# Spectra stored once and copied in DRAM, tables behind a pass's weights, and earlier copies out of PSUM in a hybrid Fourier/Hyena block on one core

## The chip, the cores and the metric

The kernel runs on one core of a Trainium2 chip. The metric is the device time of one execution in microseconds; smaller is better. Five engines work beside each other, each through its own instructions in order: TensorE (PE, matmuls), VectorE (DVE), ScalarE (ACT), GpSimd (POOL) and SyncE (SP), which here issues most of the transfers (DMAs). An engine waits where an instruction needs a result of another engine or of a transfer that is not there yet.

## The reference

One layer of an encoder on 2048 positions of 1024 channels, in float32:

```
h   = rmsnorm(x)
p   = h @ W_in                       # 2048 columns: Fourier group | x1 | x2 | v, 512 each
y_f = rmsnorm(Re(fft2(p_fourier)))   # 8 groups of 64 channels, over positions and channels
x1, x2, v = short_conv(p_rest)       # three taps over positions
k   = implicit_filters(...) * decay, normalised        # two filters per channel, both directions
z   = v
for n, gate in enumerate((x1, x2)):
    z = gate * (irfft(rfft(z) * rfft(k[:, n])) + z * d[n])
y_h = rmsnorm(z)
x   = x + concat(y_f, y_h) @ W_out
x   = x + relu(rmsnorm(x) @ W_fc1)**2 @ W_fc2
out = rmsnorm(x)
```

## The kernel before

Every product in float32 is made of three matmuls: `split` (L193) rounds an operand to a high half (ACT) and takes the rest as a low half (DVE or POOL), and `mm3` (L208) adds high x high, high x low and low x high in PSUM. So each operand of PE has an ACT cast (`wh`, `ahm`, `yh`) and a subtraction (`wl`, `alm`, `yl`) ahead of it.

The work goes in stages, one after the other on PE.

1. **Pass 1** projects x1 and x2 for 16 tiles of 128 positions and makes the short convolution; **pass 2** projects the Fourier group and v in the same way. Both are `project` (L347). `weights_in` (L314) loads a pass's weights on SP, tile by tile, and splits them. Beside pass 2 the generator `tables` (L1451) loads the tables that later stages need (`e1f`, `e1k`, `turn`, `gy`, `dk8`, `e1z`, `wo`, then `emb` and the Fourier factors `ff`) and forms sums of W_fc2 (`f` to `td`).
2. **Fourier and filters** (`fourier` L490, `filters` L539) are 44 steps. The first eleven carry the second stage of the Fourier transform: `rows(i)` (L499) negates the sine factors on ACT (`neg`), transforms one or two frequencies on PE (L510 to L516), and stores the rows. Eight filter units follow each other four steps apart. A unit generates its filter in four quarters (L584 on PE, times the decay into `k` on DVE, L589; squares on ACT, L603, added up on POOL, L607 to L610), sums over partitions (`psum_k`, L615), takes its first transform (L656, transposed by DVE into `Gk`, L660), and its second (L666), whose result `ks` goes to DRAM in four stores (`spec`, L674). `kd` holds each spectrum twice, as two halves of 64 rows. A unit in `SINGLE` stores it once, and `doubled` (L342) later copies it from DRAM to DRAM (L345). Steps 24 to 27 load `zz` (the convolved v), and `SCALE` tells at which steps DVE multiplies which pieces of it by the filters' norms (L728).
3. **Hyena** (L732): eight blocks, four groups of 128 channels for each of two gates. A block makes the transform of its input (`first`, `second`), multiplies by the spectrum (loaded as `ks`, L764), transforms back (`inverse`, `turn`: DVE transposes V into W) and multiplies by the gate (`gate`, L815). Block by block takes about 25 us. Two of the copies of `doubled` stand in blocks 1 and 2 (one spectrum each, four copies).
4. **Output projection** (`project_out` L964 with the class `Out`): per tile of positions the Fourier rows `yf` are fetched from DRAM in two loads (L917, L919), normalised (`oyn`, L237 and L995), transposed on PE (`pt_y`, L926) and multiplied. `weights` splits W_out (`ost`, into tiles G and V). Some time later the first fc1 weights are loaded into `W` (`fc1_weights`, L1103).
5. **fc1** (`fc1`, L1179): one level of a Strassen-like scheme with seven products m1 to m7 for each of 32 slices of the hidden layer, 16 slices for each half of the positions, so that after iteration 15 all operands change to the other half ("change of blocks"). `keep` (L1205) copies a PSUM sum to SBUF on ACT: `km1` (L1207, in the trace `km`), `ku2` and `ku3` (`ku`), so that the same PSUM tile can take the next product. **fc2** (L1296) has the same scheme.

What sets the order: the program is written tile by tile, and a scheduler places each engine's instructions by when their operands are ready and by priority; `tc.high_priority` moves instructions forward. `behind(later, first)` (L202) forces an instruction to be placed after another one without waiting for it. The lists `line`, `acts`, `fetched`, `stored` and `summed` hold instructions to be placed behind: `acts` the squares of the first four steps and later copies, `fetched` the last load of a spectrum.

Of the kernel before, what the change touches and what calls it, by code (L numbers as in the profile page):

```python
# [10 lines left out]
F32 = mybir.dt.float32  # L11
# [116 lines left out]
P = 128  # L128
# [6 lines left out]
def hybrid_block(ctx: ExitStack, tc: tile.TileContext, A, out):  # L135
    nc = tc.nc
# [174 lines left out]
                    yield  # L311


    def weights_in(wp, sets, stage):  # L314

        w = {}
        for h, s in enumerate(sets):
            src = wfd if s < 0 else A["w_in"][:, (1536, 512, 1024)[s] : (1536, 512, 1024)[s] + 512]
            for k in range(8):
                hi, lo = (wp.tile([P, 512], FR, tag=f"{n}{h}{k}", name=f"{n}{h}{k}") for n in ("wh", "wl"))  # L320
                pl, tag, bufs = stage[(8 * h + k) % len(stage)]
                if tag != "xt":
                    t = pl.tile([P, 512], F32, tag=tag, name="st", bufs=bufs)
                    nc.sync.dma_start(t, src[128 * k : 128 * k + 128, :])
                elif k % 2 == 0:

                    two = pl.tile([P, 2, 512], F32, tag=tag, name="st2", bufs=bufs)
                    nc.sync.dma_start(two, src[128 * k : 128 * k + 256, :].rearrange("(a p) d -> p a d", p=P))
                    t = two[:, 0]
                else:  # L330
                    t = two[:, 1]
                if s < 0:
                    split(hi, lo, t)
                else:
                    split(hi, lo, t, gmix[:, k : k + 1])
                w[h, k] = hi, lo
        return w

    line, acts, fetched, stored, summed = [], [], [], [], []
    SINGLE = (5, 7)  # L340

    def doubled(i, q):  # L342

# [146 lines left out]
    def fourier(fp, uf, e1f, ffs):  # L490
        groups = [(0,)] + [(f, f + 1) for f in range(1, 17, 2)]
        G = fp.tile([P, 128, 32, 2], F32, tag="Gf", name="Gf")
        ufv = uf.rearrange("p t (b j) -> p t b j", b=2)
        for c in range(16):
            p = pa("pf1")
            ordered(nc.tensor.matmul(p, lhsT=e1f, rhs=ufv[:, :, :, 16 * c : 16 * c + 16], start=True, stop=True))
            yield turned(G, c, p.rearrange("p (x c e) -> p c e x", c=8, e=2))

        def rows(i):  # L499

            n, p = len(groups[i]), pa("pf2")
            neg = fp.tile([P, 2, P], F32, tag="neg", name="neg", bufs=2)[:, 0:n]
            behind([nc.scalar.mul(neg, ffs[i][:, :, 1], -1.0)], acts[-1])
            for s, f in enumerate(groups[i]):
                co, si, ns = ffs[i][:, s, 0], ffs[i][:, s, 1], neg[:, s]
                a, b = p[:, 256 * s : 256 * s + 132], p[:, 256 * s + 132 : 256 * s + 256]
                gr, gi = (G[:, :, j].rearrange("p (c j) e -> p c j e", c=2) for j in (f, (16 + f) % 32))
                cos, sin = slice(0, 33), slice(33, 64)
                if f % 16 == 0:
                    ordered(nc.tensor.matmul(a, lhsT=co, rhs=gr[:, :, cos], start=True, stop=True))  # L510
                    ordered(nc.tensor.matmul(b, lhsT=ns, rhs=gr[:, :, sin], start=True, stop=True))
# [12 lines left out]
            def part(c, w):  # L524
                return row[:, :, c : c + 2 * w].rearrange("p s (c j) -> p s c j", c=2)

            nc.vector.tensor_add(part(0, 62), va[:, :, :, 0:62], sb)
            nc.vector.tensor_sub(part(132, 62), va[:, :, :, 0:62], sb)
            for c in (124, 256):
                nc.scalar.copy(part(c, 4), va[:, :, :, 62:66])  # L530
            nc.scalar.copy(row[:, :, 264:388], row[:, :, 0:124])
            nc.sync.dma_start(yfd[:, groups[i][0] : groups[i][0] + n, :], row)

        for i in range(len(groups)):
            rows(i)
            yield


    def filters(ctx, tp, fp, gp, zp, zzs, norms, emb, wo, e1k, f2, dk8, tabs, fourier_steps):  # L539
# [7 lines left out]
        class Unit:  # L547
# [3 lines left out]
            def decay(self, k):  # L551

                if k < 2:
                    decs[k] = fp.tile([P, 8, 128], F32, tag="dec", name="dec", bufs=2)
                elif k == 2:
                    two = tp.tile([P, 2, 8, 128], F32, tag="dec2", name="dec2")
                    decs[2], decs[3] = two[:, 0], two[:, 1]
                d = (nc.scalar if self.i == 0 and k < 2 else nc.sync).dma_start(decs[k], A["decay"][self.ct][:, 8 * k : 8 * k + 8, :])
                if self.i == 0 and k < 2:
                    behind([d], line[0])  # L560

            def generate(self, k):
                self.multiply(k, self.raw(k))
# [121 lines left out]
        SOLO = 11  # L685
        FOURIER = (4, 4, 4, 4, 2, 1, 1, 1, 1, 2, 1)
        LOAD = {24: 0, 25: 1, 26: 2, 27: 3}
        SCALE = {30 + 2 * j + h: [(j, 2 * h), (j, 2 * h + 1)] for j in range(4) for h in range(2)}
        for step in range(44):
            if step == SOLO:  # L690
                yield
# [40 lines left out]
    def hyena(hp, wp, rp, zz, e1, b1, f2, a2, work):  # L732
# [98 lines left out]
        for i in range(8):  # L831
            cur, old, older, new = (blocks[j] if 0 <= j < 8 else None for j in (i, i - 1, i - 2, i + 1))
            for q in range(8):
# [28 lines left out]
                if new:  # L862
                    for c in FIRSTS[q]:
                        new.first(c)
                if i in (1, 2) and q % 2:
                    doubled(SINGLE[i - 1], q // 2)
        old, older = blocks[7], blocks[6]
        for q in range(8 - LAG, 8):
            old.inverse(q)
        for k in range(0, 2):  # L870
            work.weights(hp, k)
        for q in range(4):
            older.gate(q)
        for k in range(2, 4):
            work.weights(hp, k)
        next(ahead)
        for c in range(8):
            old.turn(c)
# [10 lines left out]
    class Out:  # L889
# [20 lines left out]
        def fourier_rows(self, t, pl, tag, bufs, late=None):  # L910

            yf = pl.tile([P, 4, P], F32, tag=tag, name="yf", bufs=bufs)
            if late is not None:
                nc.scalar.copy(yf[:, 0, 0:1], late)
            src = yfd.rearrange("(b q) f c -> q f b c", b=2)
            dst = yf.rearrange("p (b n) c -> p b (n c)", b=2)
            nc.sync.dma_start(dst[0:64], src[:, t, :, 0:256])  # L917

            nc.sync.dma_start(dst[64:128], src[:, 16 - t, :, 132:388] if t else src[:, 16, :, 0:256])  # L919
            return yf.rearrange("p n c -> p (n c)")  # L920

        def parts(self, yn, yh, yl, t=0):
# [180 lines left out]
    def fc1_weights(rp, f, pair, late=None):  # L1103

        r = []
        for j, i in enumerate((f, f + 16)):
            t = rp[:, 2 * pair + j, :].rearrange("p (k f) -> p k f", k=8)
            if late is not None:
                nc.scalar.copy(t[:, 0, 0:1], late)
            nc.sync.dma_start(t, w1v[:, :, 128 * i : 128 * i + 128])  # L1110
            r.append(t)
        return r

# [65 lines left out]
    def fc1(mp, rp, zp, b, first, following, begun):  # L1179
# [24 lines left out]

        def keep(p, nm):  # L1205
            t = mp.tile([P, 512], F32, tag="keep", name=nm, bufs=4)
            nc.scalar.copy(t, p)  # L1207
            return t

        def activate(f, half, h, p, other):  # L1210
# [209 lines left out]
    with pool("ip") as ip, pool("cp1") as cp1:  # L1420
# [30 lines left out]
        def tables():  # L1451
            yield
            yield
            got.extend(load(cpool, n, [P, w], A[n]) for n, w in (("e1f", P), ("e1k", 64), ("turn", P)))
            got.append(load(cpool, "gy", [P, 8], A["g_y"]))
            got.append(cpool.tile([8, 128], F32, tag="dk8", name="dk8"))
            for n in range(2):
                nc.sync.dma_start(got[-1][4 * n : 4 * n + 4, :], A["long_d"].rearrange("a (c n) j -> n (a c) j", n=2)[n])
            f2, emb = (tp.tile([P, 32, w], F32, tag=n, name=n) for w, n in ((P, "f2"), (64, "emb")))

            second = second_weights(f2, [15, 0, 0, 1, 2, 3, 4, 5, 6, 7, 8, 9, 10, 11, 12, 13])
            got.append(load(tp, "e1z", [P, 2, P], A["e1z"]))
            got.append(load(ep, "wo", [P, 2, 512], A["filt_wo"]))
            got.extend((emb, f2))
            for f in range(0, 32, 8):
                next(second)
                yield
                if f in (0, 8):
                    next(second)
                nc.sync.dma_start(emb[:, f : f + 8], embd[:, f : f + 8])  # L1470

            for f in (1, 5, 9, 11, 13, 15):
                next(second)
# [99 lines left out]
```

## Time and profile before

| | |
|---|---|
| time, median of 3 runs | 2261.71 us (2260.7 to 2261.95) |
| profiled execution | 2262.79 us, of which the span of the trace is 2261.0 us |
| granted TensorE clock, mean | 0.993 |
| PE busy | 2199.3 us, 97% |
| DVE / ACT / POOL busy | 1475.1 / 1074.8 / 767.8 us |
| moved by DMA | 477 MB, 211 GB/s |

| stage | from, to (us) | PE busy (us) | DMA share |
|---|---|---|---|
| pass 1 | 0 to 229 | 219.87 of 229 | 0.57 |
| pass 2 | 229 to 408 | 172.53 of 179 | 0.81 |
| Fourier, filters | 408 to 589 | 167.28 of 181 | 0.76 |
| Hyena | 589 to 785 | 193.13 of 196 | 0.82 |
| output projection | 785 to 1010 | 216.41 of 225 | 0.58 |
| fc1 | 1010 to 1580 | 557.96 of 570 | 0.52 |
| fc2 | 1580 to 2261 | 672.12 of 681 | 0.64 |

A row of the trace names the line, the engine, the operation and what it writes and reads, `out<-in`, then its count, busy time and the idle time of the engine just before it with the one that ended it. "issue" is time in which the engine waited for nothing that the profile shows. The DMA share is the mean busy share of the 16 DMA engines.

### The profile page before, as it was taken

How to read it: one execution, taken by the hardware profiler on the slowest of the kernel's cores; microseconds unless marked ns; L12 is line 12 of the kernel's file. 1: busy time of each engine (PE TensorE's matmuls, PEld its weight loads, DVE VectorE, ACT ScalarE, POOL GpSimd, SP SyncE). 2: the span in 40 equal slices, each digit the busy share in tenths (PEclk: the TensorE clock that was granted, in tenths of full speed). 3: DMA queues.
4: the chain of work that ended last, by engine and by line, in shares of the span. 5: the costliest groups of instructions: out<-in, count | busy, mean ns of one | idle time of the engine just before them, and what ended most of it. 6: DMA issues, size and time to landing. Idle time of an engine off the chain costs nothing.

```text
span 2261.0 us, 34543 instructions
## 1 busy us (share of the span) xinstructions
PE 2199.3 (97%) x12881; PEld 1798.0 (80%) x12881; DVE 1475.1 (65%) x2196; ACT 1074.8 (48%) x1788; POOL 767.8 (34%) x583
## 2 busy tenths in 40 slices
PE   8999899998999989998999999999999999999998
PEld 6888788676888768887888878888888888888886
DVE  6998676776688765456444475444467666966667
ACT  6545211354456644556555565555534333533333
POOL 3434232455366502327555556555200000000000
PEclk9999999999999999999999999999999999999999
DMA  8535987579887755576444474444499666866631
GB/s 273 178 135 171 324 290 257 198 262 371 299 278 209 233 153 176 170 235 227 152 151 150 151 246 160 153 154 154 148 361 322 234 194 197 298 195 195 193 114 75
DMA packets 288953, 477.00 MB, mean 211 GB/s; under 512 B 17477, under 2 KB 133391, under 8 KB 284049
## 3 DMA queue, kind: packets, MB, share of 16 engines
q1 hardware_dynamic: 282833, 459.34, 61.1%
q10 hardware_dynamic: 5952, 15.46, 2.0%
q8 instruction: 101, 1.65, 0.3%
q14 instruction: 67, 0.55, 0.1%
HBM read 309.36 MB, written 168.00 MB: 211 GB/s over the span
## 4 chain that ended last, share of the span: by engine, by line
PE 87%; DVE 4%; DMA 3%; ACT 2%; issue 2%; POOL 1%; SPq 0%; ACTq 0%; DVEq 0%; POOLq 0%
PE p2u L212 5%; PE p2u L210 5%; PE p2u L211 5%; PE p1u L210 5%; PE p1u L212 5%; PE p1u L211 5%; PE pu L212 4%; PE pu L211 4%; PE pu L210 4%; PE p2v L212 3%; PE p2v L210 3%; PE p2v L211 3%; PE pz L778 2%; PE pk L666 2%; PE p1v L210 2%; PE p1v L212 2%
## 5 line engine op out<-in xcount | busy, mean ns | idle before, releaser
L196 ACT CAST qahm<-ra 128x1024 fp32r<-128x1024 f32 x110 | 115.9, 1053 | 345.6 <-PE p2u L211 172.0
L197 DVE TENSOR_TENSOR qalm<-ra,qahm 128x1024 fp32r<-128x1024 f32 x110 | 134.6, 1224 | 153.6 <-ACT qahm L196 151.9
L1345 POOL TENSOR_TENSOR acc<-acc,gfin 128x512 f32<-128x512 f32 x4 | 5.1, 1277 | 631.6 <-DMA out<-acc 624.4
L211 PE MATMUL pu<-wl,xh 128*128 128x512 f32 x512 | 201.5, 393 | 6.7 <-DVE wl L197 6.5
L210 PE MATMUL pu<-wh,xh 128*128 128x512 f32 x512 | 204.0, 399 | 0.4 <-ACT wh L199 0.4
L212 PE MATMUL pu<-wh,xl 128*128 128x512 f32 x512 | 201.4, 393 | 1.5 <-DVE xl L197 1.5
L211 PE MATMUL p2u<-qblm,qahm 128*128 128x512 f32 x504 | 196.1, 389 | 0.0
L210 PE MATMUL p2u<-qbhm,qahm 128*128 128x512 f32 x504 | 195.8, 389 | 0.0
L212 PE MATMUL p2u<-qbhm,qalm 128*128 128x512 f32 x504 | 195.7, 389 | 0.0
L197 DVE TENSOR_TENSOR qblm<-rb,qbhm 128x1024 fp32r<-128x1024 f32 x110 | 134.0, 1218 | 2.0 <-ACT qbhm L196 1.8
L411 POOL TENSOR_TENSOR acc<-acc,cw 128x512 f32<-128x512 f32 x45 | 60.8, 1351 | 200.9 <-DVE acc L388 197.6
L196 ACT CAST ahm<-s 128x512 fp32r<-128x512 f32 x124 | 76.7, 621 | 98.6 <-PE p1v L211 53.7
L197 POOL TENSOR_TENSOR alm<-W,ahm 128x512 fp32r<-128x512 f32 x63 | 87.8, 1395 | 97.1 <-ACT ahm L196 90.0
L211 PEld LDWEIGHTS pu<-wl,xh 128*128 128x128 f32 x512 | 97.2, 190 | 28.3 <-DVE wl L197 6.9
L196 ACT CAST qbhm<-rb 128x1024 fp32r<-128x1024 f32 x110 | 115.4, 1049 | 4.2 <-DMA rb<-in_w_fc 2.9
L212 PEld LDWEIGHTS pu<-wh,xl 128*128 128x128 f32 x512 | 97.0, 189 | 23.1 <-DVE xl L197 2.9
L210 PEld LDWEIGHTS pu<-wh,xh 128*128 128x128 f32 x512 | 97.1, 190 | 21.1 <-ACT wh L199 0.8
L210 PEld LDWEIGHTS p2u<-qbhm,qahm 128*128 128x128 f32 x504 | 94.6, 188 | 20.1 <-issue 0.3
L211 PEld LDWEIGHTS p2u<-qblm,qahm 128*128 128x128 f32 x504 | 94.6, 188 | 19.7
L212 PEld LDWEIGHTS p2u<-qbhm,qalm 128*128 128x128 f32 x504 | 94.6, 188 | 19.5
L210 PE MATMUL p1u<-bm,ahm 128*128 128x512 f32 x252 | 101.1, 401 | 8.7 <-ACT ku L1207 8.7
L196 ACT CAST ahm<-W 128x512 fp32r<-128x512 f32 x94 | 57.8, 617 | 101.7 <-PE p1u L211 99.5
(376 smaller groups left out, 6147.0 us busy)
## 6 DMA issues: line engine op xcount, KB each, us to landing
W<-in_w_fc SPq DMA_DIRECT2D x66, 512.0 KB, 4.5
ks<-spec SPq DMA_DIRECT2D x64, 512.0 KB, 4.3
rb<-td SPq DMA_DIRECT2D x64, 512.0 KB, 4.3
ra<-a1m SPq DMA_DIRECT2D x56, 512.0 KB, 3.6
ra<-a0m SPq DMA_DIRECT2D x54, 512.0 KB, 4.0
spec<-ks SPq DMA_DIRECT2D x24, 1024.0 KB, 4.9
rb<-in_w_fc SPq DMA_DIRECT2D x46, 512.0 KB, 4.7
f<-in_w_fc SPq DMA_DIRECT2D x16, 1024.0 KB, 6.7
```

Of the source, the lines that this page charges most:

```text
L196: nc.scalar.copy(hi, src)
L197: (eng or nc.vector).tensor_sub(lo, src, hi)
L210: a = nc.tensor.matmul(o, lhsT=lh, rhs=rh, start=start, stop=False, skip_group_check=more)
L211: nc.tensor.matmul(o, lhsT=lh, rhs=rl, start=False, stop=False, skip_group_check=more)
L212: return a, nc.tensor.matmul(o, lhsT=ll, rhs=rh, start=False, stop=stop, skip_group_check=more)
L411: nc.gpsimd.tensor_add(m1, m1, cw[:, 3, :])
L666: ordered(nc.tensor.matmul(p[:, 128 * j : 128 * j + 128], lhsT=f2[:, 4 * q + j, :], rhs=self.G[:, :, 4 * q + j], start=True, stop=True))
L778: nc.tensor.matmul(p[:, 256 * sp : 256 * sp + 256], lhsT=e1[:, sp, :], rhs=zz[:, :, lo : lo + 16], start=True, stop=True)
L1345: nc.gpsimd.tensor_mul(acc[i][:, c], acc[i][:, c], gfin[:, c])
```

## The change

It has seven small edits, none of which adds or removes a matmul.

- `loaded` keeps the last weight load of `weights_in`. In `tables` the loads of `e1f` to `wo` are only issued after it, and the loads of `emb`, and of the decay for unit 0's later quarters, are placed behind it.
- `rows`: the negation is placed behind `acts[5]` (the sixth recorded square) instead of the last recorded one.
- `SINGLE` is (1, 3, 5, 7) instead of (5, 7), and `doubled` runs in blocks 1 to 4 instead of 1 and 2.
- `SCALE` begins at step 33 instead of 30.
- After the last block, `weights(2)` and `weights(3)` stand ahead of the older block's gates.
- `fetched` also takes the second load of `yf`, and `fc1_weights` places its loads behind it.
- `keep` gets a raised priority.

```
+    line, acts, fetched, stored, summed, loaded = [], [], [], [], [], []
...
-                    nc.sync.dma_start(t, src[128 * k : 128 * k + 128, :])
+                    loaded[:] = [nc.sync.dma_start(t, src[128 * k : 128 * k + 128, :])]
...
-    SINGLE = (5, 7)
+    SINGLE = (1, 3, 5, 7)
...
-            behind([nc.scalar.mul(neg, ffs[i][:, :, 1], -1.0)], acts[-1])
+            behind([nc.scalar.mul(neg, ffs[i][:, :, 1], -1.0)], acts[5])
...
-                if self.i == 0 and k < 2:
-                    behind([d], line[0])
+                if self.i == 0:
+                    behind([d], line[0] if k < 2 else loaded[0])
...
-        SCALE = {30 + 2 * j + h: [(j, 2 * h), (j, 2 * h + 1)] for j in range(4) for h in range(2)}
+        SCALE = {33 + 2 * j + h: [(j, 2 * h), (j, 2 * h + 1)] for j in range(4) for h in range(2)}
...
-                if i in (1, 2) and q % 2:
+                if 1 <= i < 5 and q % 2:
                     doubled(SINGLE[i - 1], q // 2)
...
-        for k in range(0, 2):
+        for k in range(0, 4):
             work.weights(hp, k)
         for q in range(4):
             older.gate(q)
-        for k in range(2, 4):
-            work.weights(hp, k)
...
-            nc.sync.dma_start(dst[64:128], src[:, 16 - t, :, 132:388] if t else src[:, 16, :, 0:256])
+            fetched[:] = [nc.sync.dma_start(dst[64:128], src[:, 16 - t, :, 132:388] if t else src[:, 16, :, 0:256])]
...
-            nc.sync.dma_start(t, w1v[:, :, 128 * i : 128 * i + 128])
+            behind([nc.sync.dma_start(t, w1v[:, :, 128 * i : 128 * i + 128])], fetched[0])
...
-            nc.scalar.copy(t, p)
+            with tc.high_priority(offset=100):
+                nc.scalar.copy(t, p)
...
-            got.extend(load(cpool, n, [P, w], A[n]) for n, w in (("e1f", P), ("e1k", 64), ("turn", P)))
+            with tc.issue_after(loaded[0].ins):
+                got.extend(load(cpool, n, [P, w], A[n]) for n, w in (("e1f", P), ("e1k", 64), ("turn", P)))
...
-                nc.sync.dma_start(emb[:, f : f + 8], embd[:, f : f + 8])
+                behind([nc.sync.dma_start(emb[:, f : f + 8], embd[:, f : f + 8])], loaded[0])
```

Three places show how instructions move. Line numbers from L311 on differ by one or two between the two programs.

ACT where the first Fourier rows begin, before: `sqr<-k` are the squares of unit 0's third and fourth quarters (two each), `neg` the negated sine factors, `sb` the eviction of the first rows.

```order
L603 ACTIVATE sqr_3780<-k_3625 128x512
L603 ACTIVATE sqr_3783<-k_3625 128x512
L603 ACTIVATE sqr_3832<-k_3625 128x512
L603 ACTIVATE sqr_3835<-k_3625 128x512
L503 ACTIVATE neg_3841<-ff0_3612 128x128
L503 ACTIVATE neg_3855<-ff_2986 128x256
L520 COPY sb_3845<-pf2_3840 128x124
```

And with the change:

```order
L604 ACTIVATE sqr_3780<-k_3625 128x512
L604 ACTIVATE sqr_3783<-k_3625 128x512
L504 ACTIVATE neg_3841<-ff0_3612 128x128
L504 ACTIVATE neg_3855<-ff_2986 128x256
L521 COPY sb_3845<-pf2_3840 128x124
L504 ACTIVATE neg_3921<-ff_2986 128x256
L604 ACTIVATE sqr_3832<-k_3625 128x512
L604 ACTIVATE sqr_3835<-k_3625 128x512
```

Three negations and the first eviction now stand ahead of the fourth quarter's squares.

DVE at steps 30 to 33 of the filters, before: `k<-pk,dec2` makes the last unit's last quarters, `Gk` are the transposes of the first transform, `zz<-zz,norms` the products that `SCALE` places, `vk` the start of the short chain from the last unit's sum to its scale.

```order
L589 TENSOR_TENSOR k_5641<-pk_5793,dec2_5307 128x8x8x16
L660 STREAM_TRANSPOSE Gk_5614<-pk1_5833 128x8x2x32 x2
L728 TENSOR_TENSOR zz_5399<-zz_5399,norms_3598 128x4x128 x2
L589 TENSOR_TENSOR k_5641<-pk_5860,dec2_5307 128x8x8x16
L660 STREAM_TRANSPOSE Gk_5902<-pk1_5903 128x8x2x32 x2
L728 TENSOR_TENSOR zz_5399<-zz_5399,norms_3598 128x4x128 x2
L660 STREAM_TRANSPOSE Gk_5902<-pk1_5930 128x8x2x32 x2
L728 TENSOR_TENSOR zz_5399<-zz_5399,norms_3598 128x4x128 x2
L617 TENSOR_SCALAR vk_5959<-psum_k_5957 128x1
```

With the change:

```order
L590 TENSOR_TENSOR k_5641<-pk_5793,dec2_5307 128x8x8x16
L661 STREAM_TRANSPOSE Gk_5614<-pk1_5833 128x8x2x32 x2
L590 TENSOR_TENSOR k_5641<-pk_5858,dec2_5307 128x8x8x16
L661 STREAM_TRANSPOSE Gk_5900<-pk1_5901 128x8x2x32 x2
L661 STREAM_TRANSPOSE Gk_5900<-pk1_5926 128x8x2x32 x2
L618 TENSOR_SCALAR vk_5953<-psum_k_5951 128x1
```

Three pairs of products are gone from between the last quarters and the chain; the products begin behind it.

SP in the output projection, before: `ost` are loads of W_out, `W` the first of two loads of fc1's first weights, `yf` the Fourier rows of the third token, `oxt` rows of x.

```order
L898 DMA ost_8186<-in_w_out 128x1024
L898 DMA ost_8191<-in_w_out 128x1024
L1110 DMA W_8198<-in_w_fc1 128x8x128
L917 DMA yf_8244<-yfd_86 64x2x256
L919 DMA yf_8244<-yfd_86 64x2x256
L1001 DMA oxt_8293<-in_x 128x1024
```

With the change:

```order
L897 DMA ost_8194<-in_w_out 128x1024
L897 DMA ost_8199<-in_w_out 128x1024
L916 DMA yf_8252<-yfd_86 64x2x256
L918 DMA yf_8252<-yfd_86 64x2x256
L1000 DMA oxt_8301<-in_x 128x1024
```

The load of W is gone from ahead of the fetch; both loads of W now stand some 75 rows further on, behind a later fetch.

More of the change, by code (lines that the diff above doesn't have):

```diff
@@ L323, in weights_in @@
                     t = pl.tile([P, 512], F32, tag=tag, name="st", bufs=bufs)
-                    nc.sync.dma_start(t, src[128 * k : 128 * k + 128, :])
+                    loaded[:] = [nc.sync.dma_start(t, src[128 * k : 128 * k + 128, :])]
                 elif k % 2 == 0:
                     two = pl.tile([P, 2, 512], F32, tag=tag, name="st2", bufs=bufs)
-                    nc.sync.dma_start(two, src[128 * k : 128 * k + 256, :].rearrange("(a p) d -> p a d", p=P))
+                    loaded[:] = [nc.sync.dma_start(two, src[128 * k : 128 * k + 256, :].rearrange("(a p) d -> p a d", p=P))]
                     t = two[:, 0]
@@ L337, in weights_in @@
         return w
-    line, acts, fetched, stored, summed = [], [], [], [], []
-    SINGLE = (5, 7)
+    SINGLE = (1, 3, 5, 7)
     def doubled(i, q):
@@ L1453, in tables @@
             yield
-            got.extend(load(cpool, n, [P, w], A[n]) for n, w in (("e1f", P), ("e1k", 64), ("turn", P)))
[L1455 to L1459, printed above, removed]
+            with tc.issue_after(loaded[0].ins):
+                got.extend(load(cpool, n, [P, w], A[n]) for n, w in (("e1f", P), ("e1k", 64), ("turn", P)))
+                got.append(load(cpool, "gy", [P, 8], A["g_y"]))
+                got.append(cpool.tile([8, 128], F32, tag="dk8", name="dk8"))
+                for n in range(2):
+                    nc.sync.dma_start(got[-1][4 * n : 4 * n + 4, :], A["long_d"].rearrange("a (c n) j -> n (a c) j", n=2)[n])
+                f2, emb = (tp.tile([P, 32, w], F32, tag=n, name=n) for w, n in ((P, "f2"), (64, "emb")))
+                got.append(load(tp, "e1z", [P, 2, P], A["e1z"]))
+                got.append(load(ep, "wo", [P, 2, 512], A["filt_wo"]))
             second = second_weights(f2, [15, 0, 0, 1, 2, 3, 4, 5, 6, 7, 8, 9, 10, 11, 12, 13])
-            got.append(load(tp, "e1z", [P, 2, P], A["e1z"]))
-            got.append(load(ep, "wo", [P, 2, 512], A["filt_wo"]))
             got.extend((emb, f2))
```

## The prediction

> **What bounds the kernel now.** I read the page's busy times, its queues and its chain first.
>
> ```profile
> span 2261.0 us, 34543 instructions
> ...
> PE 2199.3 (97%) x12881; PEld 1798.0 (80%) x12881; DVE 1475.1 (65%) x2196; ACT 1074.8 (48%) x1788; POOL 767.8 (34%) x583
> ...
> q8 instruction: 101, 1.65, 0.3%
> ...
> PE 87%; DVE 4%; DMA 3%; ACT 2%; issue 2%; POOL 1%; SPq 0%; ACTq 0%; DVEq 0%; POOLq 0%
> ```
>
> PE is busy for 2199.3 of 2261.0 us and makes up 87% of the chain. The change adds and removes no matmul, so the 61.7 us in which PE idles, and what its clock loses behind them, are all that it can reach. Next come PE's waits: the total, how often, the longest.
>
> ```profile
> PE p1u L210 <- ACT ku L1207: 8.7, 4, 3.1
> ...
> PE pu L211 <- DVE wl L197: 6.5, 1, 6.5
> PE pk L584 <- issue: 3.9, 4, 1.6
> PE pt_y L926 <- ACT oyn L995: 3.0, 2, 2.1
> PE psum_k L615 <- POOL acc L610: 2.4, 1, 2.4
> PE pf L511 <- ACT neg L503: 2.4, 1, 2.4
> PE pk L656 <- issue: 2.2, 1, 2.2
> ...
> PE po L212 <- DVE yl L197: 1.3, 1, 1.3
> ```
>
> Each edit has one of these rows as its place. A wait can cost more than its length, as the table of windows shows (from, to, length, then PE's busy time; behind the brackets the granted clock, the DMA share and GB/s):
>
> ```profile
> 558.11:561.52 3.41, 1.51 (x14) 1.32 (x12) 3.41 (x4) 1.75 (x4) 3.18 (x3) 1.00 1.04 381
> 820.91:824.33 3.42, 1.28 (x9) 0.82 (x7) 2.42 (x11) 2.04 (x7) 0.00 (x0) 1.00 0.53 159
> 824.33:827.74 3.41, 3.41 (x12) 2.81 (x12) 1.44 (x3) 3.32 (x10) 0.00 (x0) 0.50 0.88 277
> 1319.27:1322.68 3.41, 1.31 (x6) 0.75 (x4) 2.82 (x3) 3.41 (x6) 2.71 (x3) 1.00 0.84 303
> 1322.68:1326.10 3.42, 3.34 (x8) 2.66 (x9) 3.42 (x3) 2.50 (x4) 3.42 (x2) 0.50 0.67 199
> ...
> 1010.00:1580.00 570.00, 557.96 (x2432) 458.66 (x2431) 291.25 (x320) 327.81 (x550) 338.13 (x235) 0.99 0.52 172
> ```
>
> A stretch with PE busy for 1.28 or 1.31 us is followed by one at clock 0.50; the stretch with 1.51 us (before 561.52) was not. In fc1 as a whole 2432 matmuls take 557.96 us, 0.23 each; at half clock 8 take 3.34 us, 0.42 each. So a slow stretch loses 8 x 0.19 = 1.5 us beyond the wait before it.
>
> **Pass change (tables, emb and dec behind the last weight load).** These loads leave the SP queue's early part and follow the second pass's weights. PE's 6.5 us there wait for a low half that DVE makes:
>
> ```profile
> 232.93 1.73 DVE L407 TENSOR_TENSOR acc<-acc,early 128x512 f32<-128x512 f32 x1 [1.18 <-POOL acc L415]
> ...
> 235.79 0.68 DVE L197 TENSOR_TENSOR wl<-st,wh 128x512 fp32r<-128x512 f32 x1
> ```
>
> That wl stands on DVE behind three sums, the first of which is held by POOL and not by a load; DVE's order up to it is the same afterwards. I take 0. The ends: 0, and 6.5 plus the slow stretches behind it (at least 1.5), 8.0, if a load decided after all. What moves back feeds the Fourier stage, long after.
>
> **Fourier rows (neg behind acts[5]).**
>
> ```profile
> 428.73 1.15 ACT L603 ACTIVATE sqr<-k 128x512 f32<-128x512 f32 x2 [3.57 <-DVE k L589]
> 429.50 2.62 POOL L607 TENSOR_TENSOR acc<-acc,sqr 128x512 f32<-128x512 f32 x2 [2.09 <-ACT sqr L603]
> 429.79 0.60 ACT L503 ACTIVATE neg<-ff 128x128 f32<-128x128 f32 x2
> ...
> 433.01 0.46 POOL L610 TENSOR_TENSOR acc<-acc 128x128 f32<-128x128 f32 x1
> ...
> 435.34 0.28 PE L615 MATMUL psum_k<-ones,acc 128*128 128x1 f32 x2
> ```
>
> ACT idled 3.57 us ahead of those squares; the two negs now go into that gap, and PE's 2.4 us go. Late next is POOL: PE reaches psum_k at 435.34 - 2.4 = 432.9, POOL's last sum ends at 433.47, so 0.5 is given back. I take 2.0, with 1.5 if the squares slip by a neg's length and 2.4 at best.
>
> **One stored copy of spectra 1 and 3 too (SINGLE).** Eight stores halve from 1024 to 512 KB; unit 3's four, 2 MB less, fall into the full stretch below. In the convolution eight DRAM copies of 512 KB are added: those for spectra 5 and 7 move on to blocks 3 and 4.
>
> ```profile
> 515.00:545.00 30.00, 24.85 (x571) 17.89 (x577) 16.30 (x33) 14.12 (x31) 15.15 (x14) 1.00 1.02 395
> ...
> 639.00:664.00 25.00, 25.00 (x178) 21.49 (x177) 20.82 (x33) 14.33 (x26) 15.74 (x15) 1.00 0.89 279
> 664.00:689.00 25.00, 25.00 (x178) 21.50 (x177) 21.76 (x35) 14.83 (x26) 15.99 (x15) 1.00 0.75 222
> ...
> 445.11 0.52 PE L584 MATMUL pk<-wo,emb 64*32 64x128 f32 x18 [0.96 <-issue]
> ```
>
> The added copies cost nothing: block 2 (from 639) runs with such copies at share 0.89 and PE busy 25.00 of 25.00, and block 3 at 0.75 has that room. The bytes saved: from 515 to 545 the DMA share is 1.02 at 395 GB/s, 11.8 MB, and there PE stops without a releaser. Of the 3.9 + 2.2 us of issue stops all but the 0.96 at 445 lie there, 5.1 us. I read them as PE's instruction blocks (queue q8, 1.65 MB in 101, 16 KB each) arriving late through full queues; 2 of 11.8 MB fewer shorten that. The ends: 0, if the cause is another, and 5.1. I take 3.0, a little past the middle, since a stop of this kind ends as soon as the block is in. Against it speaks the stop at 445, where the queues were far from full.
>
> The Trainium skill, "Runtime: NRT & Kernel Launch", section "Instruction fetch mechanics", has the next 16 KiB block fetched while the current one runs, with the cost of a block's end mostly hidden. By that rule the stops are no late fetch and the term is 0, the first rival below.
>
> **zz products three steps later (SCALE).**
>
> ```profile
> 552.11 3.25 DVE L728 TENSOR_TENSOR zz<-zz,norms 128x512 f32<-128x512 f32 x2
> 555.28 1.21 DVE L589 TENSOR_TENSOR k<-pk,dec 128x1024 f32<-128x1024 f32 x1
> ...
> 557.36 2.96 POOL L607 TENSOR_TENSOR acc<-acc,sqr 128x512 f32<-128x512 f32 x2 [2.55 <-ACT sqr L603]
> ...
> L728 DVE TENSOR_TENSOR zz<-zz,norms x16: 643/680/1765, 552.1 to 579.1; 128x512 f32<-128x512 f32 x16
> ...
> 590.20 2.44 DVE L480 STREAM_TRANSPOSE G<-pz 128x512 f32<-128x512 f32 x3 [8.61 <-PE pz L778]
> ```
>
> The first pair takes 3.25 us beside POOL's sums and holds back the last unit's k (555.28), from which squares, POOL's sums (557.36) and PE's psum_k follow in turn. Without it k starts up to 1.6 us earlier, when its own matmuls are done, and POOL's two sums, 2.96 here but 2.62 at 429.50, gain some tenths with the two short ones behind them. That is 2.0 to 2.4 at psum_k, and the wait of pdk behind it (0.6 us, DVE's short chain behind two transposes) goes with the new order: 2.0 to 3.0, and I take 2.8. The products then take the 0.64 to 0.68 us that most of them take already. The last six, 3.9 us, fall into DVE's idle 8.61 us ahead of the convolution; without that cover they would hold its first matmuls for 3.9.
>
> **Weight split ahead of the gates (weights 2 and 3).** PE's 1.3 us at yl go, but the transposes of W on DVE start no earlier, since they need V, and PE waits for them about that much longer. 0; at worst a slow stretch, 1.5.
>
> **yf ahead of W (fetched).**
>
> ```profile
> 813.15 0.38 SPq L1110 DMA_DIRECT2D W<-in_w_fc  x1
> ...
> 819.99 0.63 ACT L237 ACTIVATE oyn<-yf 128x512 f32<-128x512 f32 x1 [4.20 <-DMA yf<-yfd]
> ```
>
> SP stands at the load of W until its tile is free, at 813.15, with the third token's yf right behind it; ACT then idles 4.20 us for that. With W behind the fetches yf is in before ACT is, which starts at 819.99 - 4.20 = 815.8. PE's transposes also stand four matmuls earlier (0.9 us), so of the 4.2 some 3.3 are left against a wait of 2.1, less what DVE's chain of two tokens now meets in another order; I leave 0.4 of the wait: 1.7. PE is then busy over 1.5 us before 824.33 and the slow stretch goes: 1.5 more. 3.2 (0 to 3.6). W's load goes out near the last fetch, ahead of its use in fc1.
>
> **Copies of PSUM ahead in fc1 (keep).** Two of ku's four waits, 2.2 and 3.1, are those of the change of blocks:
>
> ```profile
> 1320.24 1.99 ACT L196 CAST zf<-zf 128x1024 fp32r<-128x1024 f32 x2
> 1322.14 0.57 ACT L1207 COPY ku<-p1u 128x512 f32<-128x512 f32 x1
> ...
> 1345.94 0.56 ACT L1207 COPY ku<-p1u 128x512 f32<-128x512 f32 x1
> ```
>
> The first ku goes ahead of the two zf casts, to 1320.3, which saves 2.2 + 1.5. But ACT still has the same casts to do, and the second ku comes only some 0.6 us earlier than 1345.94, so most is paid there. I take 1.0 (-1.0 to 3.7). In the other iterations the km copy moves ahead of a cast; PE has no wait there, and I take 0.
>
> **The sum.** 2.0 + 3.0 + 2.8 + 3.2 + 1.0 = 12.0. The profiled execution took 2262.8 us (span 2261.0); it would take 2250.8. It lies 1.1 above the median of 2261.7, so the forecast is 2249.7.
>
> **The rivals.**
> - *Fewer bytes bring nothing:* the issue stops stay. 12.0 - 3.0: 2252.7. For it: the stop at 445.
> - *The late waits only move:* the change of blocks is held by ACT's work, and yf's chain by DVE. 12.0 - 4.2: 2253.9.
> - *The slow stretch stays:* a lull of PE as short as 2.1 us isn't what lowers the clock, so the stretch at 824 comes anyway. 12.0 - 1.5: 2251.2. Against it: both stretches quoted follow such a lull. The Trainium skill, "TensorE: Matmul & The Clock Gate", section "The HAM clock gate", gives half rate after an idle window of about 3.4 us; by that rule a lull of 2.1 us would not do it, and the trace differs.
> - *The pass change opens too:* another 8.0: 2241.7. Against it: the row of DVE at 232.93.
> - *Slower, the km copies:* in some 31 iterations a copy of 0.57 us stands ahead of a cast that later matmuls need.
>
> ```profile
> L196 ACT CAST ahm<-W 128x512 fp32r<-128x512 f32 x94 | 57.8, 617 | 101.7 <-PE p1u L211 99.5
> ```
>
> If those had less than 0.57 us of slack, each iteration would lose up to that: 31 x 0.57 = 17.7, 2267.4. Against it: these casts themselves wait 99.5 us for PE to free their tiles, about 1 us each.
> - *Nothing that shows:* each shortened wait is given back at the next one. 2261.7.
>
> **How the numbers follow.** Forecast 0.53, fewer bytes 0.17, late waits 0.10, slow stretch 0.05, pass change 0.04, slower 0.04, nothing 0.07. The range holds the forecast and the first three rivals, 0.85 together: from 2249.7 less 5.7 (the upper ends of SINGLE and of keep with a little of the others) to 2256.5, the two dearest rivals at once (2256.9) nearly. A measurement of this kernel tells about 0.2%, 4.5 us, from no change: all cases up to 2253.9 are faster by more. Some 0.02 of them would end above 2257.2, which with "nothing" makes 0.09; slower 0.04; faster 0.87.
>
> **What would show it.** Gone from PE's waits: pf on neg, psum_k's 2.4, pt_y's 2.1, one of ku's four; issue stops of the filters at 3 us or less. Kept: pu on wl at 6.5, and PE 25.00 of 25.00 in blocks 3 and 4. I would be wrong if psum_k's wait went to pdk, if the issue stops stayed, or if PE waited for ahm in the feed-forward's iterations.

## The result and the profile after

| | before | after |
|---|---|---|
| median of 4 runs | 2261.67 us | 2248.64 us (2246.41 to 2251.65) |
| ratio | | 0.9944, 95% interval 0.9927 to 0.9961 |
| profiled execution, span | 2262.79, 2261.0 us | 2246.41, 2244.6 us |

The change makes the kernel 13.0 us faster (8.8 to 16.5 by the interval); 2249.7 had been forecast. One of the control's six runs below took 10798 us, at a granted clock of 1.0, and is left out of every number here. The profiled execution after is the quickest of the four, 2.2 us under its median, so the two traces differ by 16.4 us where the medians differ by 13.0. The page after:

```profile
span 2244.6 us, 34527 instructions
...
PE 2193.4 (98%) x12881; PEld 1794.5 (80%) x12881; DVE 1472.5 (66%) x2196; ACT 1075.1 (48%) x1788; POOL 770.8 (34%) x583
```

PE does the same 12881 matmuls. Its busy time fell by 5.9 us although nothing was taken from it. Matmuls at half clock count with their longer duration, and the trace of before has 35.8 us at clock 0.50 against 28.6 after; an estimate from this difference, half of it, is 3.6 us, and what made the rest was not looked for. The other 10.5 us of the span were idle time. PE's waits after:

```profile
PE pu L211 <- DVE wl L197: 6.5, 1, 6.5
PE p1u L210 <- ACT ku L1207: 4.6, 4, 2.8
PE pk L585 <- issue: 3.9, 3, 2.5
PE p1v L212 <- POOL alm L197: 3.0, 1, 3.0
PE p1v L210 <- DVE c L1142: 2.1, 2, 1.3
...
PE pb L815 <- DVE W L481: 1.7, 1, 1.7
PE pk L657 <- issue: 1.2, 1, 1.2
PE psum_k L616 <- POOL acc L611: 1.0, 2, 0.7
...
PE pt_y L925 <- ACT oyn L994: 0.8, 1, 0.8
...
PE po L212 <- DVE yl L197: 0.3, 1, 0.3
```

Against the list of before: pf on neg is gone, psum_k is down from 2.4 to 1.0, pt_y from 3.0 to 0.8, ku from 8.7 to 4.6. The issue stops are hardly down: 3.9 + 1.2 = 5.1 against 3.9 + 2.2 = 6.1; without the first of each, ahead of the full stretch (0.6 at 441 here, 1.0 at 445 before), 4.5 against 5.1. The wait at the pass change is the same 6.5. At the weights' edit PE's wait for `yl` is down from 1.3 to 0.3 and its wait for the transposes of W up from 0.8 to 1.7: it moved, as forecast. New are 3.0 for `alm` of POOL, 1.4 before, and 2.1 for `c` of DVE, which before's list does not have.

Because PE runs nearly the same matmuls in the same order, the traces can be cut at the same matmul of each (counted from the first), and the time from cut to cut compared. "Control" is a second trace of the changed kernel, and the last column is the trace of a kernel described below that has just that part changed.

| stretch (start in before) | before | after | control | the one part |
|---|---|---|---|---|
| first tiles of pass 1 (5) | 63.97 | 61.96 | 62.02 | tables back: 64.23 |
| pass change and most of pass 2 (219) | 188.07 | 187.90 | 189.89 | wl ahead: 181.89 |
| first Fourier rows (427) | 18.45 | 16.11 | 15.86 | neg back: 18.18 |
| filters up to the last quarter (445) | 103.53 | 103.79 | 100.35 | SINGLE back: 100.52 |
| last quarter to pdk (549) | 18.65 | 15.74 | 15.73 | SCALE back: 18.66 |
| last gates of Hyena (783) | 21.40 | 19.81 | 20.68 | |
| third token's yf (819) | 13.56 | 9.02 | 9.03 | yf back: 11.82 |
| first iterations of fc1 (1032) | 26.47 | 24.85 | 24.71 | |
| change of blocks in fc1 (1315) | 48.01 | 46.91 | 49.48 | keep back: 47.78 |

Five stretches repeat within 0.4 us between the two traces of the changed kernel; the pass change, the filters, the last gates and the change of blocks vary by 0.9 to 3.4 us from execution to execution. The first iterations of fc1 repeat in these two by chance: over all thirteen traces of this case they take 21.9 to 26.5 us, and 26.5 in both halves of the change alike (below), so the 1.7 us there are no part's price.

The places of the prediction in the trace after. The first Fourier rows: PE starts L512 before the squares of the fourth quarter are begun, and waits 0.65 us for POOL's sum, where 0.5 had been worked out.

```profile
425.43 0.38 PE L512 MATMUL pf<-Gf,neg 128*128 128x124 f32 x2
...
426.54 1.15 ACT L604 ACTIVATE sqr<-k 128x512 f32<-128x512 f32 x2
...
431.35 0.38 PE L616 MATMUL psum_k<-ones,acc 128*128 128x1 f32 x2 [0.65 <-POOL acc L611]
```

The last unit of the filters, DVE and POOL. No product stands between the quarter (549.40), the transposes and the chain (555.96). The last quarter follows the one ahead of it (545.48) by 3.9 us, and by 5.5 before (549.74 to 555.28), which is the 1.6 of the prediction; POOL's last sum follows the quarter by 5.6 us, and by 6.2 before (555.28 to 561.52).

```profile
549.40 1.22 DVE L590 TENSOR_TENSOR k<-pk,dec 128x1024 f32<-128x1024 f32 x1 [1.48 <-PE pk L585]
...
553.32 1.32 DVE L661 STREAM_TRANSPOSE Gk<-pk 128x512 f32<-128x512 f32 x2 [1.47 <-PE pk L657]
555.96 0.16 DVE L618 TENSOR_SCALAR vk<-psum_k 128x1 f32<-128x1 f32 x1 [1.33 <-PE psum_k L616]
...
558.88 1.25 DVE L729 TENSOR_TENSOR zz<-zz,norms 128x512 f32<-128x512 f32 x2
...
551.50 2.65 POOL L608 TENSOR_TENSOR acc<-acc,sqr 128x512 f32<-128x512 f32 x2 [1.28 <-ACT sqr L604]
...
555.03 0.45 POOL L611 TENSOR_TENSOR acc<-acc 128x128 f32<-128x128 f32 x1
```

The third token's yf: ACT reads it at 806.33 with no wait in front of it (4.20 us before), and PE's transposes follow at 811.35 without a wait.

```profile
806.33 0.64 ACT L237 ACTIVATE oyn<-yf 128x512 f32<-128x512 f32 x1
...
810.57 0.73 ACT L994 ACTIVATE oyn<-yf,nw_s 128x512 f32<-128x512 f32 x1 [2.48 <-DVE nw_s L225]
...
811.35 0.66 PE L925 MATMUL pt_y<-turn,oyn 128*128 128x128 f32 x4
```

The DMA share, in the windows of the filters' full stretch and of blocks 3 and 4, and from the timeline the longest issue stop:

```profile
509.00:539.00 30.00, 25.52 (x571) 18.63 (x563) 17.62 (x35) 14.66 (x31) 15.48 (x15) 0.99 1.00 373
...
655.00:680.00 25.00, 25.00 (x179) 21.49 (x178) 20.37 (x34) 14.57 (x26) 16.44 (x15) 1.00 0.94 298
680.00:705.00 25.00, 25.00 (x179) 21.50 (x178) 20.27 (x34) 14.59 (x26) 16.09 (x15) 1.00 0.92 294
```

```profile
539.03 0.43 PE L585 MATMUL pk<-wo,emb 64*32 64x128 f32 x4 [2.46 <-issue]
```

The copies are where they should be (share 0.94 and 0.92 where it was 0.75 and 0.71) and PE is busy 25.00 of 25.00. But the filters' stretch is still full, 1.00, and PE stands for 2.46 us in it.

### The profile page after: what moved, and what is told of

It reads as the page before. It is cut to its first block, busy times and chain, and to the rows that moved or that the text cites. A ratio compares the mean times of both kernels' runs of the same rounds, so it can differ in the third digit from the quotient of the medians.

```text
span 2244.6 us, 34527 instructions
## 1 busy us (share of the span) xinstructions
PE 2193.4 (98%) x12881; PEld 1794.5 (80%) x12881; DVE 1472.5 (66%) x2196; ACT 1075.1 (48%) x1788; POOL 770.8 (34%) x583
## 4 chain that ended last, share of the span: by engine, by line
PE 89%; ACT 3%; DVE 3%; POOL 2%; issue 2%; DMA 1%; SPq 0%; ACTq 0%; POOLq 0%; DVEq 0%
PE p2u L212 5%; PE p2u L211 5%; PE p2u L210 5%; PE pu L211 5%; PE pu L212 5%; PE pu L210 5%; PE p1u L210 5%; PE p1u L212 5%; PE p1u L211 5%; PE pk L667 3%; PE p2v L211 3%; PE p2v L212 3%; PE p2v L210 3%; PE pz L779 2%; PE p1v L210 2%; PE p1v L211 2%
```

## The experiments

Each edit is against the changed kernel unless said otherwise.

**Control, and three parts taken back with 3 us in question.** The control is the same program again.

> The changed kernel once more, unaltered, beside the reversals below. Both theories: 13 us below the kernel before, 2247 to 2250; its spread shows how much of a reversal can be told.

Measured: 2246.96 to 2250.65 us, median 2248.91, ratio to before 0.9942 (0.9929 to 0.9955), the same as the first time.

*Tables back* undoes the edits of `tables`, `emb` and `decay`, and with them the place of `e1z` and `wo`, which the change had moved up to the other tables:

```
-            with tc.issue_after(loaded[0].ins):
-                got.extend(load(cpool, n, ...
+            got.extend(load(cpool, n, ...
...
-                behind([nc.sync.dma_start(emb[:, f : f + 8], embd[:, f : f + 8])], loaded[0])
+                nc.sync.dma_start(emb[:, f : f + 8], embd[:, f : f + 8])
```

> The change with the tables where they stood, early in pass 1. As predicted: 0. Rival read from the trace of the changed kernel: 1.5 us longer, since two waits of PE for xl, 0.6 us at 52 and 0.9 us at 67 in the kernel before, come back when the tables' loads stand ahead of x tiles; the wait at the pass change is 6.5 us either way.

Measured: median 2253.06, ratio 0.9959 (0.9947 to 0.9971) against the control's 0.9942. Its waits of PE for xl, then the control's:

```profile
PE pu L212 <- DVE xl L197: 1.5, 2, 0.9
```

```profile
PE pu L212 <- DVE xl L197: 0.5, 1, 0.5
```

The two waits of before are back, the first 64 us take 64.23 instead of 62.02, and the wait at the pass change is 6.5 in both. So this part is worth 2.2 us, in a place that the prediction didn't look at. The intervals of the two ratios overlap; the price is read from the stretch, not from the totals.

What makes xl late stands on ACT, first with the tables back, then in the control. ACT issues two loads of `nb` (shifted rows for the convolution), at L402 and L403, and behind them it makes `xh`, which xl needs:

```profile
42.24 0.50 ACTq L402 DMA_DIRECT2D nb<-full  x1
47.05 0.79 ACTq L403 DMA_DIRECT2D nb<-full  x1
...
51.92 1.15 ACT L196 CAST xh<-xc 128x512 fp32r<-128x512 f32 x2
```

```profile
42.93 0.50 ACTq L402 DMA_DIRECT2D nb<-full  x1
43.79 0.79 ACTq L403 DMA_DIRECT2D nb<-full  x1
...
48.66 1.15 ACT L196 CAST xh<-xc 128x512 fp32r<-128x512 f32 x2
```

From the first issue to the second pass 4.81 us with the tables' loads ahead and 0.86 without, and `xh` comes 3.3 us later. Of the thirteen traces the three with the loads in their old place have 3.6 to 4.8 us there and both waits for xl (0.6 and 0.9 us), and the ten others 0.9 us and neither of the two. Why ACT's second issue stands so long behind SP's loads isn't shown; the DMA share from 40 to 44 us is 1.00 and 0.98, so full queues alone don't tell the two apart. The load of an x tile on SP, which also leaves later with the tables back (48.15 against 45.26), is not the cause of the first wait: PE waits for xl at 53.95, and transposes the next x tile only at 59.09.

*yf back* puts the loads of W ahead of the third yf again:

```
-            fetched[:] = [nc.sync.dma_start(dst[64:128], ...)]
+            nc.sync.dma_start(dst[64:128], ...)
...
-            behind([nc.sync.dma_start(t, w1v[:, :, 128 * i : 128 * i + 128])], fetched[0])
+            nc.sync.dma_start(t, w1v[:, :, 128 * i : 128 * i + 128])
```

> The change with the loads of W ahead of the third yf again. As predicted: 3.2 us longer than control, PE waits about 2 us for pt_y near 810 us. Trace of the changed kernel: 4.5 us, since hm's wait of 0.6 us goes too. Rival (the wait would have gone with the other edits): under 1 us.

Measured: median 2251.57, ratio 0.9954 (0.9942 to 0.9967), which overlaps with the control's; the stretch takes 11.82 instead of 9.03, 2.8 more.

```profile
812.98 0.63 ACT L237 ACTIVATE oyn<-yf 128x512 f32<-128x512 f32 x1 [4.02 <-DMA yf<-yfd]
...
816.76 0.66 PE L925 MATMUL pt_y<-turn,oyn 128*128 128x128 f32 x4 [1.91 <-ACT oyn L994]
...
823.32 1.06 PE L247 MATMUL pt_m<-ident,hm 128*128 128x128 f32 x8 [0.66 <-DVE hm L1018]
```

The waits are back, 1.9 and 0.7. The half clock is not: this time the lull lies across the border of two windows of the clock, and neither has as little as 1.3 us of PE in it.

```profile
812.77:816.18 3.41, 2.08 (x10) 1.38 (x8) 1.95 (x12) 1.83 (x7) 0.00 (x0) 1.00 0.97 337
816.18:819.59 3.41, 2.83 (x17) 2.49 (x18) 1.51 (x5) 3.41 (x8) 0.00 (x0) 1.00 0.59 180
```

In before the same lull was followed by a slow stretch and the piece took 13.56, 1.7 more. So yf is worth 2.8 us in any case and 1.5 to 1.7 more where the clock's windows fall so.

*SINGLE back*:

```
-    SINGLE = (1, 3, 5, 7)
+    SINGLE = (5, 7)
...
-                if 1 <= i < 5 and q % 2:
+                if i in (1, 2) and q % 2:
```

> The change with SINGLE back at (5, 7). Theory as predicted (stops come from full queues): 3.0 us longer than control, issue stops of PE in the filters some 8 us. Rival (a stop ends a fixed 1.4 us after a 16 KB instruction block has landed, and the bytes of the stores do not matter): within 0.7 us of control, stops 4 to 6 us as in both traces so far.

Measured: median 2251.82, ratio 0.9952 (0.9937 to 0.9967), which overlaps with the control's. The medians differ by 2.9, so the totals alone don't exclude the 3.0 of the prediction: the six runs spread from 2245 to 2255, and the trace is of the quickest. It has 3.0 us of issue stops, less than either expectation, the control's has 2.9, and its DMA share is full:

```profile
PE pk L585 <- issue: 3.0, 3, 1.6
```

```profile
505.00:545.00 40.00, 37.50 (x812) 26.70 (x796) 25.39 (x44) 20.00 (x43) 21.87 (x20) 1.00 1.01 394
```

The filters' stretch takes 100.52 with all the stores of before; the changed kernel had 103.79 and 100.35 in its two traces. Over all traces the stretch takes 100.35 to 105.29 us in the nine with the spectra stored once, and 103.53, 100.52 and 101.75 in the three with all the stores. So the saved bytes bring nothing that shows.

**What the issue stops are.** Where a stop ends can be set beside the record of the instruction blocks (16 KB packets of queue q8), in before, after and the control:

| kernel | block landed (us) | PE goes on (us) | between |
|---|---|---|---|
| before | 443.70 | 445.11 | 1.41 |
| before | 515.83 | 517.23 | 1.40 |
| before | 523.39 | 524.88 | 1.49 |
| before | 536.85 | 538.28 | 1.43 |
| before | 543.33 | 544.73 | 1.40 |
| after | 517.04 | 518.35 | 1.31 |
| after | 537.74 | 539.03 | 1.29 |
| control | 537.35 | 538.73 | 1.38 |

The four stops of after and the control that are not listed (at 440.58, 531.74, 442.29 and 532.27) end 1.3 to 1.5 us behind a block as well. So PE does stand for its own instructions, as the prediction read it. Whether full queues make the blocks late was tried by cutting the stores of the spectra to a quarter. The loads read that quarter twice, so this kernel leaves out three quarters of each spectrum:

```
-                    d = nc.sync.dma_start(dst, self.ks....broadcast_to([P, n, 1024]))
+                    d = nc.sync.dma_start(dst[:, :, 0:256], self.ks....broadcast_to([P, n, 1024])[:, :, 0:256])
...
-[:, :, 512 * q : 512 * q + 512]
+[:, :, 1024 * (q // 2) : 1024 * (q // 2) + 256]
```

> The change with the spectra's stores, copies and loads cut to the first quarter of each piece (the loads read that quarter twice), so it leaves out three quarters of the spectra. In the filters some 18 MB of stores are gone. Theory as predicted (stops from full queues): the issue stops of PE between 505 and 545 us fall below 1 us in all. Rival (a block takes its time from request to start whatever the queues hold, and PE stops when it runs through a block faster): 2 to 6 us of issue stops remain, each ending about 1.4 us after a block has landed, with a DMA share well below 0.9. The Hyena blocks have twice the loads here and say nothing.

Measured, in one trace, the windows and the longest stop:

```profile
445.00:505.00 60.00, 57.46 (x1304) 42.22 (x1288) 42.96 (x83) 32.12 (x79) 33.91 (x32) 1.00 0.42 136
505.00:545.00 40.00, 39.12 (x934) 28.66 (x939) 25.57 (x45) 22.45 (x48) 24.09 (x22) 1.00 0.62 219
```

```profile
480.44 0.38 PE L585 MATMUL pk<-wo,emb 64*32 64x128 f32 x4 [1.90 <-issue]
```

Between 505 and 545 only 0.9 us of stops are left, as the first theory had it; but in the emptier stretch before, at a share of 0.42, stands one of 1.90, which ends 1.5 us after its block landed at 478.96. The whole stretch takes 100.14 us, no less than the control with full queues (100.35). A stop therefore doesn't need full queues, and emptying them gained nothing against the better traces; but one trace, of a stretch that spreads over 5 us, doesn't exclude a gain of some us against the mean of the others. What sets a block's start, so that the same kernel had 5.1 us of stops in one execution and 2.9 in another, stays open.

**SCALE, neg and keep taken back, one look each.** The edits are `33 +` to `30 +`, `acts[5]` to `acts[-1]`, and `keep` without its priority.

> The change with SCALE back at step 30. As predicted: the stretch from the last quarter of the last unit to its pdk gets 2.8 us longer, with psum_k's wait of 2.4 back. Rival (the wait would move to pdk anyway): under 1 us.

Measured: the last quarter to pdk takes 18.66 instead of 15.73, 2.9, with psum_k's wait back:

```profile
PE psum_k L616 <- POOL acc L611: 3.1, 2, 2.4
```

> The change with neg behind acts[-1] again. As predicted: the first Fourier rows 2.0 us later, with PE's 2.4 us wait for neg back and psum_k's 0.7 gone. Rival (the wait is POOL's in any case): under 1 us.

Measured: the first rows take 18.18 instead of 15.86 to 16.11, 2.2. PE's wait for neg is back (the list of waits), and psum_k's wait there is gone (the timeline):

```profile
PE pf L512 <- ACT neg L504: 2.4, 1, 2.4
...
433.77 0.28 PE L616 MATMUL psum_k<-ones,acc 128*128 128x1 f32 x2
```

> The change without keep's priority. As predicted: 1.0 us longer at the change of blocks in fc1, with PE's wait of 2.2 for ku near 1306 back, and nothing in the other iterations. Rival (the copies ahead of casts cost in each iteration): fc1's other iterations get up to 18 us shorter. Second rival: the first iteration of fc1, 24.8 us for 80 matmuls with it and 26.5 before, gets 1.5 us longer too.

Measured: 47.78 us at the change of blocks, with PE's first wait for ku back (the timeline), and 7.6 in all (the list of waits) against 4.6 and 6.3 in the two traces with the priority.

```profile
PE p1u L210 <- ACT ku L1206: 7.6, 4, 3.9
```

```profile
1311.43 0.50 PE L210 MATMUL p1u<-bm,ahm 128*128 128x512 f32 x1 [2.05 <-ACT ku L1206]
```

But with the priority that stretch took 45.93 to 49.54 in the ten traces that have it (mean 47.4), without it 47.60 to 48.01 in three (mean 47.8). The wait goes, and waits for `c` of DVE (2.1 after, 4.2 in the control, 0.7 without the priority) come in its place. The iterations between the first and the change of blocks take 256.13 us in every trace, with and without: a cost in each iteration, the first rival, is out. So is the second: the first iteration takes 24.70 without the priority, no more than with it.

**The two halves.** The kernel before with the four parts that the reversals had priced:

> The kernel before with four parts alone: tables behind the weights, neg, SCALE and yf ahead of W. The reversals put these at 2.1, 2.2, 2.9 and 2.8 us, 10.0 together, with 0 to 3 more from stretches of half clock that go: 2249 to 2252. As predicted these four were 2.0 + 2.8 + 3.2 = 8.0, so 2253.7, and the other three 4.0.

Measured: 2249.82, ratio 0.9934 (0.9921 to 0.9948), 14.2 less than the kernel before in the same session, some 4 more than the four prices. And the kernel before with the other three (SINGLE, the weights ahead of the gates, keep):

> The kernel before with the other three: SINGLE, weights ahead of the gates, keep's priority. As predicted: 3.0 + 0 + 1.0 = 4.0, 2257.7. From the reversals: SINGLE nothing, keep about 0.6, so 2260 to 2261.7, no difference that the runs can tell.

Measured: ratio 1.0001 (0.9991 to 1.0010). The four carry the whole gain; the other three bring nothing that can be told, together (at most 2 us by the interval, where 4.0 had been forecast).

Each of the thirteen traces has each of the parts below either in its new or in its old place, so that the stretch of a part can be compared over all of them:

| stretch (part) | us with the part, traces | without it |
|---|---|---|
| first tiles (tables) | 61.8 to 62.9, ten | 64.0, 64.2, 64.6 |
| first Fourier rows (neg) | 15.7 to 16.3, ten | 18.5, 18.2, 19.9 |
| last quarter to pdk (SCALE) | 15.7 to 15.9, ten | 18.7, 18.7, 18.7 |
| third token's yf (yf) | 9.0, ten | 13.6, 11.8, 11.6 |
| last gates (weights) | 19.8 to 22.8, eleven | 21.4, 21.3 |

The first four part cleanly; the last gates, like the filters and the change of blocks above, do not.

**A faster one.** If the wait at the pass change is DVE's order, moving the low half ahead must open it (the edit raises the splits, the casts of the high half included):

```
                 if s < 0:
-                    split(hi, lo, t)
+                    with tc.high_priority(offset=200):
+                        split(hi, lo, t)
```

> The changed kernel with a raised priority for the splits of the second pass's first weights, which puts the last low half, wl of k = 7, ahead of the three sums on DVE. If the 6.5 us wait at the pass change is DVE's order, as predicted, it goes with the two half-clock stretches behind it, 6.5 + 2 x 1.5 = 9.5, less what is late next (the sums, xl of the first tiles): 6 to 9.5 us shorter than control, 2240 to 2243. Rival (a load or POOL decides): the wait stays above 4 us and the time within 2 us of control.

Measured: 2244.46 us, ratio to before 0.9911 (0.9897 to 0.9924), which beats both kernels, though 2240 to 2243 had been expected. DVE there:

```profile
215.55 3.04 DVE L197 TENSOR_TENSOR wl<-st,wh 128x512 fp32r<-128x512 f32 x2
...
230.63 1.76 DVE L409 TENSOR_TENSOR acc<-acc,early 128x512 f32<-128x512 f32 x1 [0.52 <-POOL acc L417]
```

The last wl stands at 215, fifteen microseconds ahead of the sums that had held it. The 6.5 us are gone, and so is the half clock (the window from 223 to 234 has clock 1.00, against 0.56 in the control from 229 to 240):

```profile
223.00:234.00 11.00, 9.80 (x44) 7.78 (x43) 10.48 (x11) 3.89 (x7) 7.74 (x6) 1.00 0.83 271
```

```profile
229.00:240.00 11.00, 5.53 (x13) 4.37 (x14) 8.21 (x12) 2.21 (x4) 3.51 (x4) 0.56 0.86 276
```

Late next are two waits for xl, 1.2 and 1.0 us:

```profile
PE pu L212 <- DVE xl L197: 2.2, 2, 1.2
```

The stretch takes 181.89 us; eleven of the other traces have 187.6 to 188.4 there and the control 189.89, so 6 less as a rule. The medians differ by 4.5, and the ratios, each to the kernel before of its own session, by 0.0031 or 7.0 us.

## Why the prediction was right

The time was right within 1.1 us, the sum 12.0 against 13.0 measured. Two of its terms were wrong and nearly cancel, 3.0 too much and 2.2 too little; that the total came so close is luck to that extent.

| part | predicted | shown |
|---|---|---|
| pass change, tables | 0 | 2.2, in pass 1 |
| Fourier rows, neg | 2.0 | 2.2 |
| one stored copy, SINGLE | 3.0 | nothing |
| SCALE | 2.8 | 2.9 |
| weights ahead of the gates | 0 | nothing: the wait moved from yl to W |
| yf ahead of W | 3.2 | 2.8, and 1.5 to 1.7 more with a slow stretch |
| keep | 1.0 | about 0.4, within the spread |

- **neg and SCALE** went as worked out: the row that waited, the engine that is late next (POOL, 0.65 us against 0.5), and the cover for the moved products. Both prices lie within 0.2 us. The prices shown add up to 10.5, and to some 12 with the slow stretch of yf; the rest of the 13.0 lies within the spread.
- **yf** had the right mechanism. The wait of 2.1 fell to none rather than to 0.4; the wait of 0.6 for hm behind it went too, which was not in the sum; and the slow stretch goes only where the clock's windows had made one.
- **SINGLE** is the step that failed: "a little past the middle, since a stop of this kind ends as soon as the block is in". That the stops end so is shown, but not that the bytes decide when the block comes. The prediction had the evidence in its own rows, the stop at 445 with the queues far from full, and gave that case 0.17. By its own sign, "if the issue stops stayed", this part was wrong: 5.1 us after against 6.1. The rule that it set against this (the Trainium skill, "Runtime: NRT & Kernel Launch", section "Instruction fetch mechanics": the fetch of the next block is mostly hidden) gives the right term, 0, but for another reason: the fetch is not hidden in the filters, it costs 2.9 to 6.1 us in the traces above, and the saved stores don't change that.
- **The tables** were priced by what waits at the place they were moved to, where 0 was right. What their loads held up at the place they left, ACT's issue of `nb` and the casts behind it, was not asked; the two waits of PE for xl (1.5 us) stood in the list of before, below the rows that were quoted.
- **keep**: the first wait opened as said and was paid again, as said; the price in each iteration, the forecast's slower case, is out by the equal 256.13 us.
- Of the rivals, "fewer bytes bring nothing" was right in its mechanism (2252.7), but the tables made up for it. The case that a 2.1 us lull doesn't lower the clock was half right: it depends on where the lull lies, by the windows above.

## What to carry to other kernels

When a load is moved, price the place it leaves as well as the place it goes to: list what stands behind it, in its own queue and on other engines that issue transfers then, and whether a short wait of the bounding engine follows there. A wait without a releaser isn't relieved by making the system emptier until its own cause has been tried alone. And where a trace shows an engine waiting behind instructions that are not urgent, as wl did behind three sums, the order on that one engine can be worth more than any single part of this change: 4 to 7 us here for one priority.

## What the runs showed of the hardware

- The twelve issue stops of before, after and the control ended 1.3 to 1.5 us after a 16 KB instruction block of PE had landed, and the 52 of all thirteen traces 0.9 to 1.6 us after one, in stretches with a DMA share of 0.42 as in those at 1.0; the filters, with their many small matmuls (64 in 1.16 us), are the only stage whose lines stand in PE's list with an issue wait.
- A lull of about 2 us is followed by 3.41 us at half clock when it falls within one window of the clock, so that PE is busy for only 1.28 or 1.31 us of it; lying across two windows (2.08 and 2.83 us busy) it is not. Equal waits thus cost 2 or 3.5 us from one execution to the next. That the windows lie on a fixed grid can be read from before: its half-clock stretches of 3.41 us begin at 786.78, 824.33, 1032.54, 1053.02, 1322.68 and 1346.57, whole multiples of 3.413 us apart. On that grid, over the thirteen traces (first 12 and last 20 us aside), half clock followed 55 of the 57 windows at full clock with PE busy under 1.5 us, and of those with over 1.6 us only two (1.87 and 1.88); between them it went both ways.
- Two traces of the same program differed by 3.4 us in the filters alone, 103.79 and 100.35, with 2.0 us more of issue stops and one slow stretch behind the longest of them (half clock from 538.7).
- An engine can stand at issuing a transfer while its own work waits behind it: ACT took 3.6 to 4.8 us from one load of `nb` to the next with SP's tables ahead, 0.9 us without, and its casts came 3.3 us later.
